# Modulation matmuls four in a row on 1024-column tiles, with loads and stores queued behind chosen weight loads

## The chip, the cores and the metric

The kernel runs on one core of a Trainium2 chip. The metric is the device time of one execution in microseconds. Three runs of the kernel before took 1499.29, 1500.6 and 1502.57 us; the median is 1500.6.

## The reference

One inference step of a two-layer decoder, for a prompt of 512 tokens and 8 sample sequences of 4 tokens. D is 1024. Each of the two layers has a mixer (layer 0: gated convolution and pooling; layer 1: dilated attention and a Conformer convolution) and a ConvFFN. Both are wrapped in RMSNorm and in a shift, scale and gate that come from the conditioning vector c. This modulation is what the change is about:

```python
c_act = jax.nn.silu(c)                       # 9 vectors: 1 prompt, 8 samples
for l in range(DEPTH):
    mod = (c_act @ w["ada_w"][l] + w["ada_b"][l])[:, None, :]   # (9,1024) @ (1024,6144)
    sh1, sc1, g1, sh2, sc2, g2 = jnp.split(mod, 6, axis=-1)
    h = _rmsnorm(x, ng[0]) * (1 + sc1) + sh1
    y, ... = _mixer_ab(h, ...)  or  _mixer_cd(h, ...)
    x = x + g1 * _rmsnorm(y, ng[1])
    h = _rmsnorm(x, ng[2]) * (1 + sc2) + sh2
    y, ... = _conv_ffn(h, ...)
    x = x + g2 * _rmsnorm(y, ng[3])
```

Beside y the outputs hold the convolution and pooling states and the key and value caches; the old cache rows are copied from input to output.

## The kernel before, in words

Activations lie feature by feature: `X`, and the normalized input split in a high and a low part, `Hhi` and `Hlo`, as [128, 8 feature blocks, 2 halves, 272 tokens] (256 prompt tokens and 16 sample tokens per half). A big product (`gemm`, `mm`, lines 527 to 531) is made of blocks of 128 output features. For each of up to 8 input blocks and each half it runs three matmuls of 272 columns: whi by Hhi, whi by Hlo, wlo by Hhi. So one block with 8 input blocks has 48 matmuls. Its weights come in loads of 256 KB into `wraw` (7 buffers, SyncE's DMA queue, line 509); ScalarE makes the high part `whi` (line 510), VectorE or GpSimd the low part `wlo` (line 511), both with 8 buffers, which is 4 blocks of 8. The first and last blocks of some products are run one half at a time.

The modulation is in `ada(l, s)`: for each layer l, a third s of the 6144 columns (2048). It runs over the 8 input blocks k. For each k there are four loads of 128 x 512 (256 KB, line 403) and four matmuls (line 404) with `cact[:, k, :]` (32 columns: 9 vectors and zeros) as the stationary operand, each into its own 32 rows of one PSUM tile. Then the result goes to SBUF (line 407), is turned by four transposes (line 410), and gets its bias and norm weight (line 412 on). 192 loads of 256 KB make up the 50 MB of `ada_w`.

`ada` is a Python generator, and `weave` takes one step of it after each block of a big product. The first third of layer 0 runs at the start, before the input projection; the other two in `mixer0` beside the input and output projections; all of layer 1 in the first ConvFFN, behind `bias_vectors`, which makes the vectors of the attention bias. The tiles of `ada` come from `wraw` at the start, then from six or four buffers of their own. The order of the trace gives priorities, from which a planner with its own costs makes a fixed order for each engine; each engine then works through its queue in that order. Nothing ties a modulation load or a matmul to a place in it.

SyncE issues all DMAs, stores too. `caches` (24 copies, DRAM to DRAM, 27 MB together, line 1207) is traced beside the last ConvFFN; having no inputs to wait for, the copies have their places wherever SyncE is free, in this trace from 103 to 916 us. The key and value stores (line 963) and the bias vectors (line 1200) stand in SyncE's queue and wait there for ScalarE.

At the start `xprep` multiplies X by its norm and `first` applies scale and shift for half 0, then `second` for half 1 after the first three blocks of half 0.

Of the kernel before, what the change touches and what calls it, by code (L numbers as in the profile page):

```python
# [41 lines left out]
XRB = 6  # L42
# [225 lines left out]
def build(nc, tc, ctx, t):  # L268
# [21 lines left out]
    cst = cp.tile([P, NCST], F32, name="cst")  # L290
    cact = cp.tile([P, KB, 32], F32, name="cact")
# [97 lines left out]
    apool = []  # L389

    def ada_tile():
        if apool:
            ap, n = apool[-1]
            return ap.tile([P, CH, HT], F32, name="adaw", bufs=n).rearrange("p a n -> p (a n)")[:, 0:512]
        return wp.tile([P, 512], F32, name="adaw", tag="wraw", bufs=WRAW)

    def ada(l, s):
        ps = psum1("psada")
        for k in range(KB):
            for j in range(4):  # L400
                wt = ada_tile()
# [6 lines left out]
        pt = psum1("psadat")  # L408
# [3 lines left out]
        V.tensor_tensor(  # L412
            mods[l][:, s * 16:s * 16 + 16, :].rearrange("p (j c) n -> p j c n", c=4),
            pt.rearrange("p (c j n) -> p j c n", c=4, j=4)[:, :, :, 0:NMOD],
            par[:, o:o + 16].rearrange("p (j c) -> p j c", c=4).unsqueeze(3).to_broadcast([P, 4, 4, NMOD]),
            op=ADD)

        def ng(i):
            oo = PAR["norm_g"][0] + (l * 4 + i) * KB
            return par[:, oo:oo + KB].unsqueeze(2).to_broadcast([P, KB, NMOD])  # L420

        mb = mods[l]
        if s == 0:
            V.scalar_tensor_tensor(cA[l][0], mb[:, 8:16, :], 1.0, ng(0), op0=ADD, op1=M)
        elif s == 1:
            V.tensor_tensor(cG[l][0], mb[:, 16:24, :], ng(1), op=M)
        else:
            V.scalar_tensor_tensor(cA[l][1], mb[:, 32:40, :], 1.0, ng(2), op0=ADD, op1=M)
            V.tensor_tensor(cG[l][1], mb[:, 40:48, :], ng(3), op=M)
        yield  # L430
# [73 lines left out]
    def load_w(ap, kc, eng):  # L504
# [3 lines left out]
        n = kc * P  # L508
        SY.dma_start(raw[:, :n], ap.rearrange("p k n -> p (k n)"))
# [4 lines left out]
    def load_block(w, n, k0, k1, eng):  # L514
        out = []
        for a in range(k0, k1, 4):
            b = min(a + 4, k1)
            hi, lo = load_w(w[n, :, a:b, :], b - a, eng[a // 4 % 2])
            out += [(hi[:, i * P:(i + 1) * P], lo[:, i * P:(i + 1) * P]) for i in range(b - a)]
        return out  # L520

    def mm(ps, wt, src, h0, h1):
        last = len(wt) - 1
        for i, (whi, wlo) in enumerate(wt):
# [5 lines left out]
            for h in range(h0, h1):  # L530
                PE.matmul(ps[:, h, :HT], wlo, xhi[:, h, :], start=False, stop=(i == last))  # L531
# [86 lines left out]
    def ffn(l, nxt, side, pre):  # L618
# [11 lines left out]
        if l == 0:  # L630
            apool.append((fp, 4))
# [42 lines left out]
        def body():  # L674
# [8 lines left out]
            SY.dma_start(t[f"o_f{l}"], so)  # L683
            yield from down(ng - 1)
            apool.clear()
# [8 lines left out]
    def mixer0(nxt, side, pre, loaded):  # L694
# [5 lines left out]
        apool.append((st0, XRB))  # L700
# [42 lines left out]
        def ev(i, nb, ps, h0, h1):  # L743
            kind, j = divmod(nb, 4)
            if kind == 3:
# [5 lines left out]
                if h1 == 2:  # L751
# [4 lines left out]
                    if j == 3:  # L756
                        SY.dma_start(t["o_b"], ob)
# [6 lines left out]
            elif kind == 2:  # L764
# [5 lines left out]
                z = ap_.tile([P, 562], F32, name="za", bufs=2)  # L770
                conv3(z, ext, pr("a_w")[:, 3 * j:3 * j + 3])
                tmp["z"] = z
            else:
# [7 lines left out]
        weave(gemm(t["w_abi"], order, 0, KB, srcH, ev, lead=LEAD0, mids=(pre, None), loaded=loaded), side, drain=False)  # L781
        SY.dma_start(t["o_a"], oa)
        ea.close()
        er.close()
        apool[-1] = (es.enter_context(pool("mix0w")), 4)
        ey = ExitStack()
        Y = ey.enter_context(pool("mix0y", side="right")).tile([P, KB, 2, HT], F32, name="Y0")
        weave(gemm(t["w_abo"], range(KB), 0, KB, lambda k: (yhi[:, k], ylo[:, k]),
                   out_evac(Y, acc, cG[0][0], True, True), tail=TAIL, mids=(None, lambda: junction(0, Y, acc, nxt))), side)
        es.close()  # L790
        apool.clear()
# [3 lines left out]
    def mixer1(nxt, pre):  # L795
# [41 lines left out]
        def ev_d(i, nb, ps, h0, h1):  # L837
# [12 lines left out]
            if h1 == 2:  # L850
                SY.dma_start(t["o_d"][:, j, 1:9, :], sv[:, :, 4:34])
                SY.dma_start(t["o_d"][:, j, 0, :], ext[:, 512:542])
# [84 lines left out]
        def ev_c(i, nb, ps, h0, h1):  # L937
# [25 lines left out]
            SY.dma_start(t["o_kv"][6 * (kind - 1) + n], kt)  # L963
# [226 lines left out]
    def bias_vectors():  # L1190

        rel = ada_tile()[0:64, 0:12]
        SY.dma_start(rel, t["rel"])
        for c in range(3):
            oh, rv = ada_tile()[0:64, :], ada_tile()[0:12, :]
            SY.dma_start(oh, t["ohp"][:, c * 512:(c + 1) * 512])
            ps = psum1("psrv")
            PE.matmul(ps[0:12, :], rel, oh, start=True, stop=True)
            A.activation(rv, ps[0:12, :], AF.Copy)
            SY.dma_start(rvd[:, c * 512:(c + 1) * 512], rv)  # L1200
            yield

    def caches():
        for g in range(3):
            n = CBATCH[g]
            for b in range(0, DB, n):
                SY.dma_start(t[f"o_c{g}"][b:b + n].rearrange("b w n -> b (w n)").rearrange("b (q n) -> q b n", q=16),
                             t[f"cache{g}"][b:b + n, 4:CW[g]].rearrange("b w n -> b (w n)").rearrange("b (q n) -> q b n", q=16))
# [4 lines left out]
    er = ExitStack()  # L1213
# [74 lines left out]
```

## Time and profile before

| | us |
|---|---|
| median of three runs | 1500.6 |
| profiled execution, device time | 1496.0 |
| its span | 1494.3 |
| TensorE busy | 1417.8 |
| VectorE, ScalarE, GpSimd busy | 882.1, 618.8, 170.6 |
| modulation matmuls (line 404) busy | 102.6 |

The span runs from the first to the last instruction. In the rows below an engine is named PE (TensorE matmul), PEld (its weight loads), DVE (VectorE), ACT (ScalarE), POOL (GpSimd) or SP (SyncE); a "q" behind it is its queue, and L404 is line 404 of the kernel. One fp32 matmul is two instructions. In timelines and in the chain, the first number is the start, the second the time taken, and x is the number of instructions. In rows by stretch, each engine's busy time stands with its count; the last three numbers are the granted TensorE clock as a share of full speed, the share of time for which the 16 DMA engines were busy, and what they moved.

### The profile page before, as it was taken

Reading aid. Unit: us, or ns where it says so; the run is one execution under the profiler, and the core shown is the slowest. Engines: PE = TensorE matmul, PEld = TensorE weight load, DVE = VectorE, ACT = ScalarE, POOL = GpSimd, SP = SyncE. Lnnn points to the kernel's source line nnn. Section 1 sums busy time; section 2 is a strip of 40 time slices with the busy share of each in tenths; the row PEclk is TensorE's granted clock in tenths of the full one; section 3 lists DMA queues with packets and bytes.
Section 4 is the critical chain, followed back from the end, with each engine's and each line's share of the span. In section 5 each row is a group of like instructions: output and inputs, shape, how many; then the busy total and the mean of one; then the engine's idle time right before and its main releaser. Section 6 shows DMA issues by size and latency. Waiting matters only on the chain.

```text
span 1494.3 us, 26853 instructions
## 1 busy us (share of the span) xinstructions
PE 1417.8 (95%) x10354; PEld 1271.0 (85%) x10354; DVE 882.1 (59%) x1788; ACT 618.8 (41%) x1145; POOL 170.6 (11%) x384
## 2 busy tenths in 40 slices
PE   6899997999999999999799999999699999999995
PEld 2578897988798798899699999678599999999995
DVE  1664427753165346446859979652886456456457
ACT  2322235743244234235652442643674444244244
POOL 0210014110011001001500000000521011011011
PEclk9799998999999999999999999999899999999998
DMA  7775633325445546544236245446122332332311
GB/s 264 242 253 187 201 106 100 103 98 180 160 155 194 161 139 212 165 158 186 89 113 197 94 141 178 135 146 239 57 85 69 103 93 71 104 91 65 113 51 61
DMA packets 112633, 207.72 MB, mean 139 GB/s; under 512 B 20884, under 2 KB 33684, under 8 KB 111992
## 3 DMA queue, kind: packets, MB, share of 16 engines
q1 hardware_dynamic: 112504, 206.00, 42.5%
q8 instruction: 81, 1.33, 0.4%
q14 instruction: 48, 0.39, 0.1%
HBM read 198.63 MB, written 34.39 MB: 156 GB/s over the span
## 4 chain that ended last, share of the span: by engine, by line
PE 88%; DVE 6%; DMA 2%; ACT 2%; issue 1%; SPq 0%; POOL 0%; POOLq 0%; DVEq 0%; ACTq 0%
PE psmm L527 23%; PE psmm L531 23%; PE psmm L529 23%; PE psada L404 6%; PE psn L442 2%; PE psmh L529 2%; PE psmh L527 2%; PE psmh L531 2%; PE pso L1013 1%; PE psl L979 1%; PE psl L981 1%; DVE X L492 1%; DVE Yf L491 1%; DVE Y L491 1%; DVE Hlo L481 1%
## 5 line engine op out<-in xcount | busy, mean ns | idle before, releaser
L510 ACT ACTIVATE whi<-wraw 128x512 fp32r<-128x512 f32 (+1 forms) x404 | 239.8, 600 | 511.4 <-PE psmm L529 411.6
L527 PE MATMUL psmm<-Hhi,whi 128*128 128x272 f32 x2028 | 435.9, 291 | 1.0 <-DVE extu L750 1.0
L531 PE MATMUL psmm<-Hhi,wlo 128*128 128x272 f32 x2028 | 431.4, 289 | 0.3 <-POOL wlo L511 0.3
L529 PE MATMUL psmm<-Hlo,whi 128*128 128x272 f32 x2028 | 430.0, 288 | 0.0
L511 DVE TENSOR_TENSOR wlo<-wraw,whi 128x512 fp32r<-128x512 f32 (+1 forms) x374 | 240.8, 649 | 303.4 <-ACT whi L510 288.3
L527 PEld LDWEIGHTS psmm<-Hhi,whi 128*128 128x128 f32 x2028 | 321.4, 189 | 24.3 <-issue 12.6
L529 PEld LDWEIGHTS psmm<-Hlo,whi 128*128 128x128 f32 x2028 | 322.5, 189 | 9.0 <-issue 9.0
L531 PEld LDWEIGHTS psmm<-Hhi,wlo 128*128 128x128 f32 x2028 | 321.5, 189 | 9.9 <-issue 9.2
L527 PE MATMUL psmm<-act_hi,whi 128*128 128x272 f32 x624 | 135.5, 290 | 0.0
L531 PE MATMUL psmm<-act_hi,wlo 128*128 128x272 f32 x624 | 135.3, 289 | 0.0
L529 PE MATMUL psmm<-act_lo,whi 128*128 128x272 f32 x624 | 132.7, 288 | 0.0
L578 DVE SCALAR_TENSOR_TENSOR fz<-fext,par,fz 128x560 f32<-128x560 f32 x88 | 70.5, 801 | 74.3 <-ACT fz L577 74.2
L404 PE MATMUL psada<-adaw,cact 128*32 128x512 f32 x384 | 102.6, 628 | 8.3 <-DMA adaw<-ada_w 8.3
L527 PEld LDWEIGHTS psmm<-act_hi,whi 128*128 128x128 f32 x624 | 99.6, 188 | 11.8 <-issue 8.4
L531 PEld LDWEIGHTS psmm<-act_hi,wlo 128*128 128x128 f32 x624 | 99.6, 188 | 7.6 <-issue 7.5
L529 PEld LDWEIGHTS psmm<-act_lo,whi 128*128 128x128 f32 x624 | 99.1, 188 | 0.8 <-issue 0.8
L577 ACT ACTIVATE fz<-fext,par 128x560 f32<-128x560 f32 x88 | 75.2, 855 | 34.5 <-DVE fext L647 34.5
L874 DVE SCALAR_TENSOR_TENSOR zd<-extd,par,zd 128x512 f32<-128x512 f32 x120 | 87.0, 746 | 0.7
L569 POOL COPY fso<-fext 128x2 f32<-128x2 f32 x88 | 23.1, 263 | 530.6 <-ACT fext L646 530.6
L579 DVE SCALAR_TENSOR_TENSOR fz<-fext,par,fz 128x560 f32<-128x560 f32 x88 | 70.5, 801 | 2.7
L646 ACT ACTIVATE fext<-psmm 128x512 f32<-128x512 f32 (+1 forms) x88 | 49.7, 564 | 51.1 <-PE psmm L531 51.1
L527 PE MATMUL psmh<-Hhi,whi 128*128 128x272 f32 x148 | 48.2, 326 | 16.1 <-ACT Hhi L479 14.5
(260 smaller groups left out, 1692.9 us busy)
## 6 DMA issues: line engine op xcount, KB each, us to landing
adaw<-ada_w SPq DMA_DIRECT2D x192, 256.0 KB, 3.6
wraw<-w_up SPq DMA_DIRECT2D x176, 256.0 KB, 3.0
wraw<-w_dn SPq DMA_DIRECT2D x64, 256.0 KB, 2.8
o_c<-cache SPq DMA_DIRECT2D x8, 2040.0 KB, 10.0
wraw<-w_cdi SPq DMA_DIRECT2D x52, 256.0 KB, 4.6
wraw<-w_abi SPq DMA_DIRECT2D x32, 256.0 KB, 4.5
o_c<-cache SPq DMA_DIRECT2D x8, 1016.0 KB, 7.1
kc<-kc SPq DMA_DIRECT2D x28, 256.0 KB, 3.7
```

Of the source, the lines that this page charges most:

```text
L404: PE.matmul(ps[32 * j:32 * j + 32, :], cact[:, k, :], wt, start=(k == 0), stop=(k == KB - 1))
L442: PE.matmul(ps, ones, a, start=(i == 0), stop=(i == n - 1))
L510: A.activation(hi[:, :n], raw[:, :n], AF.Copy)
L511: eng.tensor_tensor(lo[:, :n], raw[:, :n], hi[:, :n], op=SUB)
L527: PE.matmul(ps[:, h, :HT], whi, xhi[:, h, :], start=(i == 0), stop=False)
L529: PE.matmul(ps[:, h, :HT], whi, xlo[:, h, :], start=False, stop=False)
L531: PE.matmul(ps[:, h, :HT], wlo, xhi[:, h, :], start=False, stop=(i == last))
L577: A.activation(z[:, :n], ext[:, 2:2 + n], AF.Identity, bias=b, scale=w[:, 2:3])
L578: V.scalar_tensor_tensor(z[:, :n], ext[:, 1:1 + n], w[:, 1:2], z[:, :n], op0=M, op1=ADD)
L579: V.scalar_tensor_tensor(z[:, :n], ext[:, 0:n], w[:, 0:1], z[:, :n], op0=M, op1=ADD)
L646: A.activation(fpr(ext, 2, h0, h1), cpr(ps, h0, h1), AF.Copy)
L874: V.scalar_tensor_tensor(cpr(z), ip, dw[:, i:i + 1], cpr(z), op0=M, op1=ADD)
```

## The change

The parts of the diff, in order. `ada` works on halves (l, s, q) of 256 columns per matmul. One load of 512 KB brings four operands, [128, 2, 512]; there are 96 such loads in place of 192. The four matmuls are traced together, and `issue_after(newest[0])` puts them behind the last matmul of the newest block. The tiles have four buffers (start and mixer 0) or three (first ConvFFN). Evacuation and bias go by halves, and the four transposes become two matmuls with a selection of 36 columns, `ssel`. `queued()` puts a DMA behind the newest weight load: modulation loads, bias inputs, cache copies and state stores. The projections' weaving is new: in mixer 0 two tiles per step, all beside the input projection; in the ConvFFN one tile, with 4 steps for 3 tiles; cache copies every third step. The key and value stores and the bias vectors are issued by ScalarE. At the start the normalized X lies in the norm's four buffers, for half 1 made in `second`'s place.

```diff
-XRB = 6
+ADB = (4, 3)
...
+    ssel = cp.tile([P, 4, NMOD], F32, name="ssel")
+    apool = [st0]
+    newest, loaded_w = [], []
+    def queued():
+        return tc.issue_after(loaded_w[0]) if loaded_w else nullcontext()
     def ada_tile():
-        if apool:
-            ap, n = apool[-1]
-            return ap.tile([P, CH, HT], F32, name="adaw", bufs=n).rearrange("p a n -> p (a n)")[:, 0:512]
-        return wp.tile([P, 512], F32, name="adaw", tag="wraw", bufs=WRAW)
-    def ada(l, s):
-        ps = psum1("psada")
-        for k in range(KB):
-            for j in range(4):
-                wt = ada_tile()
-                o = s * 2048 + j * 512
-                SY.dma_start(wt, t["ada_w"][l, k, :, o:o + 512])
-                PE.matmul(ps[32 * j:32 * j + 32, :], cact[:, k, :], wt, start=(k == 0), stop=(k == KB - 1))
-            yield
-        ev = np_.tile([P, 512], F32, name="adaev", tag="nsq", bufs=NSQ)
+        return apool[-1].tile([P, 2, 512], F32, name="adaw", bufs=ADB[len(apool) - 1])
+    def ada(halves, per, ahead):
+        todo = [(l, s, q, k) for l, s, q in halves for k in range(KB)]
+        tiles = []
+        def load():
+            if todo[len(tiles):]:
+                l, s, q, k = todo[len(tiles)]
+                tiles.append(ada_tile())
+                with queued():
+                    SY.dma_start(tiles[-1], t["ada_w"][l].rearrange("k p (s a q n) -> s q k p a n", s=3, a=2, q=2)[s, q, k])
+        for _ in range(ahead):
+            load()
+        for i, (l, s, q, k) in enumerate(todo):
+            load()
+            if k == 0:
+                ps = psum1("psada")[:, 0:256]
+            wt = tiles[i]
+            with tc.issue_after(newest[0]) if newest else nullcontext():
+                for j in range(4):
+                    PE.matmul(ps[32 * j:32 * j + 32, :], cact[:, k, :], wt[:, j // 2, 256 * (j % 2):256 * (j % 2) + 256],
+                              start=(k == 0), stop=(k == KB - 1))
+            if k == KB - 1:
+                ada_out(l, s, q, ps)
+            if i % per == per - 1:
+                yield
+    def ada_out(l, s, q, ps):
+        if q == 0 and l == 0 and s == 0:
+            V.tensor_copy(ssel, ident.rearrange("p (j n) -> p j n", j=4)[:, :, 0:NMOD])
+        ev = wp.tile([P, 256], F32, name="adaev", tag="wraw", bufs=WRAW)
         A.activation(ev, ps, AF.Copy)
-        for c in range(4):
-            PE.transpose(pt[:, c * P:(c + 1) * P], ev[:, c * P:(c + 1) * P], ident)
+        for c in range(2):
+            PE.matmul(pt[:, :, c, :], ev[:, c * P:c * P + P], ssel, start=True, stop=True)
...
-        SY.dma_start(raw[:, :n], ap.rearrange("p k n -> p (k n)"))
+        loaded_w[:] = [SY.dma_start(raw[:, :n], ap).ins]
...
-                PE.matmul(ps[:, h, :HT], wlo, xhi[:, h, :], start=False, stop=(i == last))
+                x = PE.matmul(ps[:, h, :HT], wlo, xhi[:, h, :], start=False, stop=(i == last))
+        newest[:] = [x.ins]
...
-            SY.dma_start(t["o_kv"][6 * (kind - 1) + n], kt)
+            A.dma_start(t["o_kv"][6 * (kind - 1) + n], kt)
...
+            A.dma_start(rvd[:, c * 512:(c + 1) * 512], rv[c])
...
+                with queued():
+                    SY.dma_start(t[f"o_c{g}"][b:b + n]...
...
+            XR[h, c] = np_.tile([P, CH, HT], F32, name="xr", tag="nsq", bufs=NSQ)
...
-    a = ada(0, 0)
+    a = ada([(0, 0, 0), (0, 0, 1)], 2, 2)
...
-    pre = mixer0((0, 1), chain(delay(1), pace(chain(ada(0, 1), ada(0, 2)), 7, 8)),
-                 second, loaded)
-    pre = ffn(0, (1, 0), chain(delay(8), bias_vectors(), slow(chain(ada(1, 0), ada(1, 1), ada(1, 2)), 2)), pre)
+    pre = mixer0((0, 1), chain(delay(1), ada([(0, i, q) for i in (1, 2) for q in range(2)], 2, 0)),
+                 lambda: (xprep(1), first(1, 0, KB)), loaded)
+    pre = ffn(0, (1, 0), chain(delay(8), bias_vectors(), pace(ada([(1, i, q) for i in range(3) for q in range(2)], 1, 0), 3, 4)), pre)
     pre = mixer1((1, 1), pre)
-    ffn(1, None, caches(), pre)()
+    ffn(1, None, slow(caches(), 3), pre)()
```

## Rows read from the trace of the kernel before

**Rows 1.** The page, parts 1 and 4: span, TensorE's busy time, chain by line.
```profile
span 1494.3 us, 26853 instructions
PE 1417.8 (95%) x10354; PEld 1271.0 (85%) x10354; DVE 882.1 (59%) x1788; ACT 618.8 (41%) x1145; POOL 170.6 (11%) x384
PE psmm L527 23%; PE psmm L531 23%; PE psmm L529 23%; PE psada L404 6%; PE psn L442 2%; PE psmh L529 2%; PE psmh L527 2%; PE psmh L531 2%; PE pso L1013 1%; PE psl L979 1%; PE psl L981 1%; DVE X L492 1%; DVE Yf L491 1%; DVE Y L491 1%; DVE Hlo L481 1%
```

**Rows 2.** TensorE's waits: line <- releaser: us in total, times, longest.
```profile
PE psada L404 <- DMA adaw<-ada_w: 8.3, 3, 4.1
...
PE psmm L531 <- POOL wlo L511: 0.3, 1, 0.3
```

**Rows 3.** Line 404 by stretch: length, PE, PEld busy (count), clock, DMA share, GB/s.
```profile
61.30:195.00 133.70, 27.49 (x128) 3.89 (x128) 1.00 0.65 212
325.00:640.00 315.00, 51.84 (x192) 7.17 (x192) 1.00 0.53 175
```

**Rows 4.** TensorE's timeline from 61 us, line 404: first and last of 75.
```profile
61.35 1.06 PE L404 MATMUL psada<-adaw,cact 128*32 128x512 f32 x6
...
637.13 1.07 PE L404 MATMUL psada<-adaw,cact 128*32 128x512 f32 x8
```

**Rows 5.** Chain of waits from 110 us: start, us, work, instructions in it.
```profile
117.47 0.99 PE psada L404 x8
118.46 0.45 PE psmm L527 x2
118.91 0.25 PE psmm L529 x2
...
124.64 0.44 PE psadat L410 x4
```

**Rows 6.** The same chain from 334 us: one modulation matmul alone.
```profile
334.68 0.97 PE psada L404 x2
335.66 0.32 PE psmm L529
```

**Rows 7.** The same chain from 1026 us: 256-column matmuls of the sample attention.
```profile
1026.44 0.57 PE psr L1157 x8
1027.01 0.45 PE psmm L527 x2
...
1033.78 1.00 PE psr L1157 x16
...
1035.98 0.80 PE psys L1168 x8
```

**Rows 8.** Stretches: length, PE, PEld, DVE, ACT, POOL, clock, DMA share, GB/s.
```profile
2.00:22.00 20.00, 15.05 (x40) 4.37 (x40) 0.00 (x0) 4.44 (x9) 0.00 (x0) 1.00 1.03 351
22.00:34.00 12.00, 9.28 (x38) 3.55 (x38) 6.43 (x12) 3.01 (x6) 0.00 (x0) 1.00 0.45 145
34.00:47.50 13.50, 8.25 (x22) 1.97 (x22) 1.69 (x11) 2.79 (x5) 3.60 (x7) 0.75 0.94 325
47.50:61.30 13.80, 10.94 (x48) 9.54 (x48) 13.24 (x39) 8.63 (x18) 5.53 (x4) 0.63 0.54 174
1100.00:1456.00 356.00, 356.00 (x2858) 356.00 (x2857) 206.26 (x385) 155.26 (x250) 42.77 (x127) 1.00 0.30 88
```

**Rows 9.** SyncE's timeline: modulation loads issued around 18 us.
```profile
17.93 14.28 SPq L403 DMA_DIRECT2D adaw<-ada_w  x8
```

**Rows 10.** VectorE's timeline: two products of X and its norm for half 1.
```profile
64.25 1.36 DVE L1224 TENSOR_TENSOR xr<-X,nr 128x544 f32<-128x544 f32 x2 [1.06 <-PE psada L404]
```

**Rows 11.** Waits of SyncE's queue: line <- releaser: us, times, longest.
```profile
SPq L403 <- PE psada L404: 243.7, 80, 22.4
...
SPq L963 <- ACT kt L960: 75.0, 12, 17.5
```

**Rows 12.** DMA issues by line: count, KB each, median us to landing.
```profile
vc<-vc SPq DMA_DIRECT2D x14, 512.0 KB, 6.9
```

**Rows 13.** Line 963, issue of the key and value stores: ns min/median/max, first and last start.
```profile
L963 SPq DMA_DIRECT2D o_kv<-kt x12: 332/338/352, 760.8 to 921.1; - x12
```

More of the change, by code (lines that the diff above doesn't have):

```diff
@@ L682, in body @@
                 yield from up(e + 1, FGROUPS[gi + 1][1])
-            SY.dma_start(t[f"o_f{l}"], so)
-            yield from down(ng - 1)
-            apool.clear()
+            for i, _ in enumerate(down(ng - 1)):
+                if i == 3:
+                    with queued():
+                        SY.dma_start(t[f"o_f{l}"], so)
+                yield
+            del apool[1:]
         weave(body(), side)
@@ L780, in mixer0 @@
         order = ABI
-        weave(gemm(t["w_abi"], order, 0, KB, srcH, ev, lead=LEAD0, mids=(pre, None), loaded=loaded), side, drain=False)
-        SY.dma_start(t["o_a"], oa)
+        weave(gemm(t["w_abi"], order, 0, KB, srcH, ev, lead=LEAD0, mids=(pre, None), loaded=loaded), side)
+        with queued():
+            SY.dma_start(t["o_b"], ob)
+            SY.dma_start(t["o_a"], oa)
         ea.close()
         er.close()
-        apool[-1] = (es.enter_context(pool("mix0w")), 4)
         ey = ExitStack()
         Y = ey.enter_context(pool("mix0y", side="right")).tile([P, KB, 2, HT], F32, name="Y0")
-        weave(gemm(t["w_abo"], range(KB), 0, KB, lambda k: (yhi[:, k], ylo[:, k]),
-                   out_evac(Y, acc, cG[0][0], True, True), tail=TAIL, mids=(None, lambda: junction(0, Y, acc, nxt))), side)
+        for _ in (gemm(t["w_abo"], range(KB), 0, KB, lambda k: (yhi[:, k], ylo[:, k]),
+                   out_evac(Y, acc, cG[0][0], True, True), tail=TAIL, mids=(None, lambda: junction(0, Y, acc, nxt)))):
+            pass
         es.close()
-        apool.clear()
         return lambda: (junction(1, Y, acc, nxt), ey.close())
@@ L1190, in bias_vectors @@
     def bias_vectors():
-        rel = ada_tile()[0:64, 0:12]
-        SY.dma_start(rel, t["rel"])
+        bt = [ada_tile() for _ in range(3)]
+        rel, rv = bt[1][0:64, 1, 0:12], [bt[2][0:12, 0, :], bt[2][0:12, 1, :]]
+        with queued():
+            SY.dma_start(bt[0][0:64], t["ohp"][:, 0:1024].rearrange("p (a n) -> p a n", a=2))
+            SY.dma_start(bt[1][0:64, 0, :], t["ohp"][:, 1024:1536])
+            SY.dma_start(rel, t["rel"])
+        yield
+        yield
+        rv.append(ada_tile()[0:12, 0, :])
         for c in range(3):
-            oh, rv = ada_tile()[0:64, :], ada_tile()[0:12, :]
-            SY.dma_start(oh, t["ohp"][:, c * 512:(c + 1) * 512])
             ps = psum1("psrv")
-            PE.matmul(ps[0:12, :], rel, oh, start=True, stop=True)
-            A.activation(rv, ps[0:12, :], AF.Copy)
-            SY.dma_start(rvd[:, c * 512:(c + 1) * 512], rv)
+            with tc.issue_after(newest[0]):
+                PE.matmul(ps[0:12, :], rel, bt[c // 2][0:64, c % 2, :], start=True, stop=True)
+            A.activation(rv[c], ps[0:12, :], AF.Copy)
+            A.dma_start(rvd[:, c * 512:(c + 1) * 512], rv[c])
             yield
@@ L1212, in build, with xstat, xprep @@
     warm(cact[:, 0, 0:1])
-    er = ExitStack()
-    st0 = er.enter_context(pool("mix0r", side="right"))
     XR = {}
-    def xprep(h, c0, c1):
-        if c0 == 0:
-            XR[h] = rstd(squares(h), onesD)
-        r = XR[h].unsqueeze(1).to_broadcast([P, CH, HT])
-        for c in range(c0, c1, CH):
-            XR[h, c] = st0.tile([P, CH, HT], F32, name="xr", tag="adaw", bufs=XRB)
+    def xstat(h):
+        XR[h] = rstd(squares(h), onesD)
+    def xprep(h):
+        r = XR.pop(h).unsqueeze(1).to_broadcast([P, CH, HT])
+        for c in range(0, KB, CH):
+            XR[h, c] = np_.tile([P, CH, HT], F32, name="xr", tag="nsq", bufs=NSQ)
             V.tensor_tensor(XR[h, c], X[:, c:c + CH, h, :], r, op=M)
```

66 lines of the change are left out of this document (29 added, 37 removed).

## The prediction

> **What bounds the kernel now.** I read the page's parts 1 and 4 first: TensorE is busy 1417.8 us of a 1494.3 us span, and the chain that ended last lies on it for 88%, of which 6% is line 404, the modulation matmuls [rows 1]. So what a matmul takes is paid almost in full, and a faster DMA or vector step pays only where TensorE idles. TensorE's own waits come second. Modulation matmuls wait 8.3 us in 3 places for their weights, and the big products wait 0.3 us for a split weight [rows 2]: behind the start nothing that SyncE loads is late. Third, line 404 by stretch: 128 of its 384 instructions lie in layer 0's input projection and 192 in layer 0's ConvFFN, in both of which the granted clock is 1.00 [rows 3]; the other 64 belong to the start. Last, the start: the DMA engines move 351 GB/s up to 22 us, only 145 GB/s from there to 34, and 325 up to 47.5; then, up to 61.3 us, TensorE runs 48 matmul records where a full stream at 0.125 us each (two take 0.25 [rows 5]) would need 6.0 of 13.8 us [rows 8].
>
> **What one modulation batch costs.** Four matmuls of 32 output columns each use separate column groups and run side by side. Eight instructions (four matmuls in a row) take 0.99 us on the chain, and the pair of big matmuls behind them takes 0.45 instead of 0.25 [rows 5]: 1.19 us. A single one takes 0.97, and the matmul behind it 0.32 instead of 0.125 [rows 6]: 1.17 us. One alone costs what four cost. After the start the timeline has 75 such batches, from 61.35 to 637.13 us [rows 4], for 160 matmuls: 20 are whole fours, 5 are threes, 15 pairs and 35 single ones. 26 lie in the input projection, 49 in the ConvFFN. At 1.18 us that is 88.5 us.
>
> **The change, part by part.**
> *Four in a row, 256 columns each.* One 512 KB tile now holds the four operands, so all four become ready together, and the order to stand behind a block's last matmul keeps them from cutting into it. After the 16 batches of the start there are 80. The nearest rows are the sample attention's, with the same 32-column groups and the same 256 moving columns: a four takes 0.57 and the pair behind it 0.45, so 0.77 us; two fours in a row take 1.00, so 1.20 with the pair behind [rows 7]. In the ConvFFN one batch goes at a time: 48 x 0.77 = 37.0 us. In the input projection two go per step: 16 x 1.20 = 19.2. Together 56.2 us, a gain of 32.3. Were no two adjacent, 80 x 0.77 = 61.6, gain 26.9. Were a 256-column four as dear as today's 1.17, 93.6, a loss of 5.1; I take the rows with the same shape.
> *The fold.* Four transposes (0.44 us [rows 5]) become two matmuls of 36 columns per half, 10 pairs behind the start where 5 fours stood. Four matmuls of 16 columns take 0.80 [rows 7], so a pair about 0.40, plus 0.1 for the change of shape: 10 x 0.50 - 5 x 0.44 = +2.8 us. Ends: 0, and +10 if a pair costs as much as 1.2 us. The halved evacuations (12 on ScalarE, more small adds on VectorE) lie beside matmuls; those engines are busy 41% and 59% [rows 1].
> *The start.* The hole from 22 to 34 us is TensorE's doing: eight loads take 14.28 us to issue [rows 9], as each waits for a buffer that a lone matmul (1 us) must free, with the norm's matmuls in between. Now a batch frees 512 KB in well under the 1.5 us that 512 KB takes at 351 GB/s, so the loads set the pace. The 13.1 MB moved up to 47.5 us (20 x 351 + 12 x 145 + 13.5 x 325, in GB/s times us [rows 8]) would take 37.5 us at 351, 8 us less. The first half's modulation is done eight tiles earlier, so half of the first pre-norm work can come before the end of the loads: I take 2 of the 7.8 us lost after 47.5. Against it, half 1's normalized X loses two of its early buffers: two more products, 1.36 us [rows 10], and some reshuffling, -2. Sum -8 us. Ends: 0 (the hole stays, filled by other waits) and -16 (all 8 and all 7.8).
> *Loads pinned behind weight loads.* In SyncE's queue, in order, whatever stands behind a load that waits for its buffer waits too. Today such waits come to 243.7 us [rows 11] and TensorE feels none of it. With four buffers and two tiles per step, a modulation load can go two blocks ahead: 2 x (48 x 0.125 + 1.2) = 14.4 us, of which the next block's weights, queued behind it, need 6.9 us to land, as a 512 KB load does [rows 12], and some 3 us to be split: some 5 us spare. The traffic is 1.57 MB per 7.2 us, 218 GB/s, against 212 now [rows 3] and 351 shown [rows 8]. In the ConvFFN three tiles at 4/3 blocks each give four blocks, over 20 us. I charge 2 us for hiccups; ends 0, and 35 if each of the 64 steps is late by 0.55.
> *Cache copies into the last ConvFFN, state stores later.* 27 MB move into a stretch in which TensorE is busy 356.0 of 356 us and DMA stands at 0.30 [rows 8]: some 90 GB/s more over 72 of its 88 steps, on top of 88. Taking them away elsewhere frees nothing TensorE waits for. 0 us; if their cover fails, weight loads there come late.
> *ScalarE's own stores.* SyncE's queue stood 75.0 us for 12 of them [rows 11]; nobody on TensorE waited. 15 issues of about 0.34 us [rows 13] go to ScalarE, with evacuations queued behind them; exposed in full that is 5 us, beside matmuls 0.
> Sum: -32.3 + 2.8 - 8 + 2 = -35.5 us. The profiled execution took 1496.0 us (span 1494.3 and 1.7 around it), so 1460.5 for its like; the median of the runs shown is 1500.6, so the forecast is 1465.
>
> **A rule weighed.** The granted clock was 0.75 from 34 to 47.5 us and 0.63 behind it, a mix of 2.4 and 1.2 GHz; in the first of these stretches TensorE was busy 8.25 of 13.5 us [rows 8]. The Trainium skill, "TensorE: Matmul & The Clock Gate", section "HAM oscillation", says that short bursts between DMA waits bring the slow clock back each time, and it speaks against this change: a TensorE that is faster in the start idles more there. In direction this trace agrees, by the two clocks just named. By my sum the start gives 8 us; by the rule it gives about 4 (rival 2).
>
> **Rivals.**
> 1. *Pinned loads become the bound.* Place: SyncE's queue in the input projection, where the spare is 5 us and VectorE splits weights between other work. A weight late by x costs x in each step; from 0.55 us per step over 64 steps the gain is gone. At 1 us a step: 1465 + 64 - 2 = 1527, slower. Against: 0.3 us of weight waits today [rows 2], traffic hardly above today's. 7%.
> 2. *The start gives little.* Either TensorE goes through the start at 1.2 GHz: the first three blocks' 72 matmuls would cost 9 us more at half clock, of which the 13.8 us at a mean of 0.63 already hold some 5, so 4 lost, 1469; or the norm's matmuls still block the batches, 1473. For it: the norm's squares wait for X as before. 20%.
> 3. *The start gives all.* -16 instead of -8: 1457. For it: VectorE works 13.24 of the 13.8 us behind the loads [rows 8], and half of that could move ahead. 10%.
> 4. *The change doesn't do what it says:* something readier is put between the four. Split in two, 160 x 0.77 = 123 us instead of 56: 1532. Against: one load wakes all four. 3%.
>
> **How the numbers follow.** The forecast (gains of line 404 and the start near the sum) has 60%: 1465, its own range 1458 to 1473. Rivals 2 and 3 lie beside it, rivals 1 and 4 are slower (10%, of which 2% may be no change at a mild lateness). The range takes the lower end from rival 3 and the unpaired batches with little from the start (1465 + 5.4 + 8) plus some lateness as the upper: 1452 to 1483. Faster than 0.2% (3 us, about what a measurement can tell from no change) 0.90, within it 0.02, slower 0.08.
>
> **What would show it.** Line 404 after the start: 48 lone groups of eight instructions near 0.57 us and 16 pairs near 1.00, none of two instructions. The last modulation load landing near 37 to 40 us, with no hole in GB/s. TensorE's waits still without DMA or weight rows beyond a few us. The last ConvFFN still at full business. Wrong would be: rows of line 404 waiting for DMA behind the start, matmuls waiting for wlo or whi, batches near 1 us each, or an input projection that is not some 10 us and a ConvFFN that is not some 20 us shorter.

## The result and the profile after

The changed kernel takes 1577.7 us (median of 4 runs, 1576.4 to 1578.9) against 1499.9 for the kernel before: ratio 1.0519, 95% interval 1.0497 to 1.0541. It is 78 us slower; 1465 was forecast, 35 us faster.

The page's span and busy times of the changed kernel:

```profile
span 1575.8 us, 27444 instructions
PE 1432.6 (91%) x10762; PEld 1319.8 (84%) x10762; DVE 885.2 (56%) x1803; ACT 612.1 (39%) x1151; POOL 159.2 (10%) x384
```

TensorE is busy 15 us more than before [rows 1], but 143 us of the span are idle, where it was 76. Its own waits, the first by total and the modulation's:

```profile
PE psmm L554 <- ACT whi L537: 38.6, 12, 4.9
PE psmm L558 <- DVE wlo L538: 19.3, 23, 1.2
...
PE psada L426 <- DMA adaw<-ada_w: 11.4, 10, 5.4
PE psadat L440 <- ACT adaev L437: 11.3, 11, 3.5
```

The split weights, for which TensorE waited 0.3 us before [rows 2], now cost 58 us. No load stands beside them: all of line 426's waits for loads lie before 38 us.

For the stages I cut each kernel at five marks: the first pooling matmul of the input projection, and the first normalized product of each junction (VectorE's Y from Y and nr). Lengths in us:

| | start | first mixer | first ConvFFN | second mixer | last ConvFFN | median |
|---|---|---|---|---|---|---|
| before | 82.3 | 146.0 | 487.0 | 338.3 | 417.7 | 1499.9 |
| changed | 66.5 | 150.8 | 484.3 | 349.6 | 501.8 | 1577.7 |

Behind the last mark some 23 us follow in both. The marks do not cut the work alike: in the changed kernel 40 records of big matmuls fewer lie in the first ConvFFN (3172, before 3212) and 40 more in the second mixer. At 0.125 us each that is 5 us. At equal work the first ConvFFN is 2.3 us longer than before, not 2.7 shorter, and the second mixer 6.3 us longer, not 11.3. Stage lengths below are by the marks; "at equal work" says that they were set right in this way.

The loss lies in the last ConvFFN, +84.1 us: the stage in which the forecast put nothing but the cache copies, at 0 us. The stretches of the changed kernel (columns as in [rows 8]) are the start, most of the first mixer and of the first ConvFFN, and of the last:

```profile
0.00:22.00 22.00, 10.88 (x69) 3.39 (x70) 0.31 (x3) 5.96 (x9) 0.46 (x9) 1.00 0.94 319
22.00:34.00 12.00, 11.38 (x80) 6.70 (x79) 6.88 (x19) 5.68 (x10) 0.00 (x0) 1.00 0.85 288
34.00:47.50 13.50, 6.52 (x38) 4.64 (x35) 12.80 (x40) 6.89 (x14) 5.06 (x8) 0.62 1.03 381
...
66.50:217.20 150.70, 145.58 (x1211) 133.71 (x1211) 65.30 (x131) 43.95 (x81) 11.19 (x21) 0.99 0.50 168
...
290.00:701.50 411.50, 399.59 (x3187) 367.45 (x3186) 199.14 (x393) 148.61 (x258) 26.78 (x112) 0.98 0.42 135
...
1100.00:1553.00 453.00, 402.58 (x2961) 395.80 (x2960) 215.56 (x421) 159.66 (x272) 34.19 (x127) 0.92 0.37 126
```

In the last row TensorE is idle for 50.4 us, and its granted clock is 0.92. Before, the same work (1100 to 1471 us) was 370.9 busy of 371.2 at 1.00. So of the 84 us 50 are idle and 32 are slower matmuls.

How one stop comes about shows in ScalarE's timeline of the changed kernel (start, duration, instruction, in brackets the idle time before it and who ended it):

```profile
1212.42 0.60 ACT L674 ACTIVATE fext<-psmm 128x512 f32<-128x512 f32 x1 [4.13 <-PE psmm L558]
1213.41 0.85 ACT L605 ACTIVATE fz<-fext,par 128x560 f32<-128x560 f32 x1 [0.39 <-DVE fext L675]
1215.97 0.67 ACT L686 ACTIVATE fz<-fz 128x560 f32<-128x560 f32 x1 [1.71 <-DVE fz L607]
1216.55 3.21 ACT L537 ACTIVATE whi<-wraw 128x512 fp32r<-128x512 f32 x6
```

and in TensorE's beside it:

```profile
1211.92 0.40 PE L558 MATMUL psmm<-Hhi,wlo 128*128 128x272 f32 x2
1217.21 0.82 PE L554 MATMUL psmm<-Hhi,whi 128*128 128x272 f32 x2 [4.89 <-ACT whi L537]
...
1219.36 0.82 PE L558 MATMUL psmm<-Hhi,wlo 128*128 128x272 f32 x2 [0.87 <-DVE wlo L538]
```

Six splits of weights (3.21 us) stand in ScalarE's queue behind the evacuation, convolution and gate of the block that TensorE has just finished. Their data is there: nothing stands in brackets. TensorE can't start the next block until that whole evacuation is through. ScalarE meanwhile waits 4.13 us for TensorE, with the six splits behind the waiting instruction. It happens ten times (37.0 of the 38.6 us), five times for 4.9 us and five times for 2.5, mostly some 25 us apart. VectorE's low parts stand in sixes too, and TensorE waits 13.1 us in 15 places of that stage for them. Loads do come late to ScalarE there, which they did not in the kernel before (its waits from 1051.2 to 1553 us):

```profile
ACT whi L537 <- DMA wraw<-w_dn: 16.2, 6, 4.6
ACT whi L537 <- DMA wraw<-w_up: 6.8, 3, 5.2
```

But all nine of these waits lie between the stops, while TensorE works; none of the ten stops has one in it. In the kernel before the same engine takes its splits singly, between the evacuations:

```profile
1136.71 0.85 ACT L577 ACTIVATE fz<-fext,par 128x560 f32<-128x560 f32 x1 [0.56 <-DVE fext L647]
1138.01 0.63 ACT L510 ACTIVATE whi<-wraw 128x512 fp32r<-128x512 f32 x1 [0.45 <-PE psmm L529]
1141.00 0.63 ACT L510 ACTIVATE whi<-wraw 128x512 fp32r<-128x512 f32 x1 [2.35 <-PE psmm L529]
1141.54 0.58 ACT L646 ACTIVATE fext<-psmm 128x512 f32<-128x512 f32 x1
```

After each of the ten stops the clock is at 0.50, the lower of its two levels (1.2 and 2.4 GHz). Stretches of the changed kernel around the first:

```profile
1213.00:1217.00 4.00, 0.00 (x0) 0.00 (x0) 2.12 (x4) 1.90 (x4) 0.58 (x3) 0.72 0.00 2
1217.00:1219.00 2.00, 1.28 (x4) 0.95 (x4) 1.97 (x6) 2.00 (x5) 0.00 (x0) 0.50 0.00 0
...
1221.00:1223.00 2.00, 2.00 (x11) 2.00 (x10) 1.32 (x3) 0.00 (x0) 0.00 (x0) 0.50 0.90 259
1223.00:1225.00 2.00, 2.00 (x11) 2.00 (x11) 0.00 (x0) 0.00 (x0) 0.00 (x0) 0.50 0.99 264
1225.00:1227.00 2.00, 2.00 (x18) 2.00 (x18) 0.00 (x0) 0.00 (x0) 0.00 (x0) 1.00 1.47 580
```

From 1221 to 1225 us a 2 us stretch holds 11 matmuls instead of 18. Behind the ten stops TensorE works for 3 to 8 us at 0.50; the 32 us are some 3 us for each stop. The Trainium skill, "TensorE: Matmul & The Clock Gate", section "HAM oscillation", says of a kernel whose matmuls wait for DMAs that after each such wait they start at the slow clock again. Here the waits are for ScalarE's splits; this trace agrees, at 0.50.

### The profile page after: what moved, and what is told of

Read it like the earlier page. It is cut to its first block, busy times and chain, and to the rows that moved or that the text cites. A ratio compares the mean times of both kernels' runs of the same rounds, so it can differ in the third digit from the quotient of the medians.

```text
span 1575.8 us, 27444 instructions
## 1 busy us (share of the span) xinstructions
PE 1432.6 (91%) x10762; PEld 1319.8 (84%) x10762; DVE 885.2 (56%) x1803; ACT 612.1 (39%) x1151; POOL 159.2 (10%) x384
## 4 chain that ended last, share of the span: by engine, by line
PE 82%; DVE 10%; ACT 4%; DMA 2%; issue 1%; POOL 0%; SPq 0%; DVEq 0%; POOLq 0%; ACTq 0%
PE psmm L558 22%; PE psmm L554 22%; PE psmm L556 21%; PE psada L426 3%; PE psn L469 3%; PE psmh L554 2%; PE psmh L556 1%; PE psmh L558 1%; PE pso L1043 1%; DVE wlo L538 1%; DMA kc<-kc 1%; PE psl L1009 1%; PE psl L1011 1%; DVE X L519 1%; ACT fz L605 1%
## 5 line engine op out<-in xcount | busy, mean ns | idle before, releaser
L554 PE MATMUL psmm<-Hhi,whi 128*128 128x272 f32 x2028 | 450.3, 299 | 33.7 <-ACT whi L537 33.7
L558 PE MATMUL psmm<-Hhi,wlo 128*128 128x272 f32 x2028 | 444.0, 296 | 13.5 <-DVE wlo L538 13.5
L556 PE MATMUL psmm<-Hlo,whi 128*128 128x272 f32 x2028 | 442.3, 295 | 0.0
L554 PEld LDWEIGHTS psmm<-Hhi,whi 128*128 128x128 f32 x2028 | 334.3, 196 | 55.2 <-ACT whi L537 37.1
L558 PEld LDWEIGHTS psmm<-Hhi,wlo 128*128 128x128 f32 x2028 | 333.9, 195 | 19.1 <-DVE wlo L538 17.6
L556 PEld LDWEIGHTS psmm<-Hlo,whi 128*128 128x128 f32 x2028 | 334.5, 195 | 1.6 <-issue 1.4
L606 DVE SCALAR_TENSOR_TENSOR fz<-fext,par,fz 128x560 f32<-128x560 f32 x88 | 70.5, 801 | 70.8 <-ACT fz L605 70.5
L675 DVE COPY fext<-psmm 128x32 f32<-128x32 f32 (+1 forms) x88 | 16.5, 188 | 142.2 <-ACT fext L674 140.9
L605 ACT ACTIVATE fz<-fext,par 128x560 f32<-128x560 f32 x88 | 75.2, 854 | 28.6 <-DVE fext L675 27.8
L621 DVE TENSOR_TENSOR Yf<-psmm,Yf 128x544 f32<-128x544 f32 x32 | 23.2, 724 | 89.1 <-PE psmm L558 89.1
L426 PE MATMUL psada<-adaw,cact 128*32 128x256 f32 x768 | 61.7, 412 | 11.4 <-DMA adaw<-ada_w 11.4
```

What stands on the lines that cost most here:

```text
L426: PE.matmul(ps[32 * j:32 * j + 32, :], cact[:, k, :], wt[:, j // 2, 256 * (j % 2):256 * (j % 2) + 256], start=(k == 0), stop=(k == KB - 1))
L554: PE.matmul(ps[:, h, :HT], whi, xhi[:, h, :], start=(i == 0), stop=False)
L556: PE.matmul(ps[:, h, :HT], whi, xlo[:, h, :], start=False, stop=False)
L558: x = PE.matmul(ps[:, h, :HT], wlo, xhi[:, h, :], start=False, stop=(i == last))
L605: A.activation(z[:, :n], ext[:, 2:2 + n], AF.Identity, bias=b, scale=w[:, 2:3])
L606: V.scalar_tensor_tensor(z[:, :n], ext[:, 1:1 + n], w[:, 1:2], z[:, :n], op0=M, op1=ADD)
```

## The experiments

Theory A: the cache copies, queued behind chosen weight loads, change the order of ScalarE's instructions in the last ConvFFN, which is fixed before the run, and this order alone is the loss. Rival B: the copies' bytes make the weight loads there late. Rival C: another part of the change does it.

**1. The pinned copies alone.**

```diff
 before.py
+    with queued():                     # behind the newest weight load
         SY.dma_start(t[f"o_c{g}"]..., t[f"cache{g}"]...)
-    ffn(1, None, caches(), pre)()
+    ffn(1, None, slow(caches(), 3), pre)()
```

> The kernel before with one part of the change: the 24 cache copies go behind weight loads in SyncE's queue, one in three steps of the last ConvFFN. Theory A (order: the planner prices a 2 MB copy as a long stop of SyncE's queue, takes the six weight loads behind it for late, and fixes ScalarE's order with their splits behind the next blocks' evacuations; TensorE then waits for that order): the last ConvFFN takes 453 us instead of 371, total 1500 + 82 = 1582. Theory B (traffic: the copies' bytes hold up the weight loads on the chip): the same 1582. Theory C (the loss comes from another part, such as the modulation edits or ScalarE's own stores): 1500.

Measured: 1550.3 us, ratio 1.0335 (1.0313 to 1.0356). The last ConvFFN takes 503.4 us (+85.7) and shows the same ten stops, so C is out for that stage. TensorE's waits for whi there:

```profile
PE psmm L531 <- ACT whi L514: 37.0, 10, 4.9
```

The total is 32 us under the 1582 expected, for the first ConvFFN takes 454.0, 33 less than before (30 at equal work), with the modulation code untouched. Its line 408 in the stretch of the second row of [rows 3]:

```profile
325.00:640.00 315.00, 23.44 (x176) 3.46 (x176) 1.00 0.49 154
```

23.4 us where there were 51.8 (the other 16 instructions lie before 325 us). In the order of TensorE's instructions all 24 groups of four matmuls in that stage are now whole; before, 49 batches did the same work. So it was the copies, spread over that stage in the kernel before, that had taken the fours apart. 25 batches less, at the forecast's 1.18 us, are 29.5 us, which is the 30 at equal work.

**2. The change with its copies as before.**

```diff
 after.py
-    with queued():
-        SY.dma_start(t[f"o_c{g}"]..., t[f"cache{g}"]...)
+    SY.dma_start(t[f"o_c{g}"]..., t[f"cache{g}"]...)
-    ffn(1, None, slow(caches(), 3), pre)()
+    ffn(1, None, caches(), pre)()
```

> The changed kernel with the copies traced as in the kernel before: not pinned, one per step. A and B: the last ConvFFN is back at 371 us, total 1577.7 - 82 = 1496. C: 1577. If the copies, now placed by the planner into the first ConvFFN, put splits late there too (four bunches of seven in ScalarE's order), up to 15 us of that are lost again: 1496 to 1511.

Measured: 1499.8 us, ratio 0.9998 (0.9983 to 1.0013); last ConvFFN 418.7. The pinned copies are the whole 78 us, and with the copies where they were the rest of the change is worth nothing.

**3. The copies in the same stretch from GpSimd's queue.**

```diff
 after.py
-    with queued():
-        SY.dma_start(t[f"o_c{g}"]...
+    with tc.issue_after(newest_g[0]):  # GpSimd's newest state store
+        G.dma_start(t[f"o_c{g}"]...
```

> The changed kernel with the same copies in the same stretch, but issued by GpSimd, each behind its latest state store; ScalarE's order then has the splits in ones and twos again. This tells A from B: the bytes stay in the last ConvFFN, the order doesn't. A: the last ConvFFN at 371 to 380 us, total 1496 to 1505. B: still near 453 us, total 1570 to 1580.

Measured: 1536.8 us, ratio 1.0245 (1.0224 to 1.0267); last ConvFFN 464.4: between what was expected of A and of B. With the same bytes there TensorE waits for no weight any more, which speaks against B. Half of the loss stays, under other names (waits of TensorE in that stage):

```profile
PE psmm L554 <- DVE fext L675: 12.8, 5, 7.2
PE psmm L554 <- DVE act_hi L610: 11.6, 2, 5.8
PE psmh L554 <- DVE act_hi L610: 6.1, 2, 5.2
```

They wait for evacuations now. GpSimd fills the state rows that these need, and its queue holds the copies' issues too. That this is the link I infer; no run parts it.

**4. The splits ahead of the evacuations, copies as in the change.**

```diff
 after.py, gemm(), in the last ConvFFN only
+    for n in range(i, i + 4): wts[n] = load_block(...)   # three blocks ahead
     mm(ps, wts.pop(i), src, 0, 2)
+    with tc.issue_after(loaded_a[0]), tc.issue_after(loaded_v[0]):
         evac(i, blocks[i], ps, 0, 2)   # behind the newest split
```

> The changed kernel with the copies where they are, in SyncE's queue, but in the last ConvFFN the weights of three blocks ahead are traced first, and a block's evacuation is tied behind the newest split on ScalarE and VectorE. Only the order is changed; queue and bytes stay. A: most of the waits go, the ConvFFN at 375 to 400 us, total 1498 to 1523 (bunches stay where a product begins). B: weights still land late and TensorE waits for them with a DMA row behind it, total 1560 or more.

Measured: 1540.1 us, ratio 1.0267 (1.0243 to 1.0291); last ConvFFN 463.2: again between A and B. The waits for whi fall to 24.3 us in five places from 37.0 in ten, and the stage loses 45.5 us instead of 84.1. Five stops in place of ten leave about half the loss.

**5 and 6. The copies in the second mixer**, issued by GpSimd, in the changed kernel and in the kernel before.

```diff
-    SY.dma_start(t[f"o_c{g}"]...
+    with tc.issue_after(G.tensor_copy(cpin, newhi[0][:, 0:1]).ins):
+        G.dma_start(t[f"o_c{g}"]...
-    pre = mixer1((1, 1), pre)
+    pre = mixer1((1, 1), pre, pace(caches(), 5, 4))
     ...
+    ffn(1, None, iter(()), pre)()
```

> The changed kernel, but its cache copies are issued by GpSimd, each behind the newest weight load, in the second mixer and no longer in the last ConvFFN, whose weight splits then stand in the order of the kernel before. If the order of the splits is the whole loss of the last ConvFFN, that stage takes 418 us (before 417.7, changed kernel 501.8) and the kernel 66.6 + 151 + 484 + 348 + 418 + 23 = 1490 us. If another part of the change costs in that stage too, it stays at 430 us or more and the time at 1505 or more. If the copies' 16.8 MB themselves cost where they run, the second mixer is longer than 360 us.

> The kernel before, with the cache copies alone moved: issued by GpSimd in the second mixer, so that they break neither the fours of the ada batches in the first ConvFFN nor the order of the splits in the last. If whole fours are worth what the pinned copies alone showed there (first ConvFFN 487 to 454 us), the kernel takes 1499 - 33 = 1466 us, with the last ConvFFN at 418. If that gain came from somewhere else than the copies' leaving the first ConvFFN, it stays at 1499.

(The copies are 27 MB, eight each of 2040, 1016 and 248 KB, not the 16.8 given there.) Measured: 1558.1 us, ratio 1.0383 (1.0363 to 1.0403), and 1529.9, ratio 1.0208 (1.0185 to 1.0232): both misses in the total. The last ConvFFN is right (419.9 and 418.9), the first too (483.9 and 456.9), but the second mixer takes 410.1 and 403.0, which is 60.5 and 64.7 us more than in the two kernels without the move; a cost of the copies where they run was the third case of 5. In experiment 6:

```profile
PE pssl L1071 <- DMA kc<-kc: 21.5, 9, 5.4
PE psvt L934 <- ACT kt L961: 19.3, 1, 19.3
```

Here transfers do come late: TensorE waits for the key caches themselves, which it waited 1.7 us for before. So the copies have a price in this stage, where a product reads its loads directly. Why kt comes late in the second row no run parts.

**7. As 5, with the fold one step later.**

```diff
+    if late and k == late[1]:
+        ada_out(*late[0]); late = None
     if k == KB - 1:
-        ada_out(l, s, q, ps)
+        late = ((l, s, q, ps), per - 1)   # the start's two halves stay as they were
```

> As the changed kernel with its copies in the second mixer, and each fold of an ada half (ScalarE's copy, the four small matmuls, VectorE's additions) comes one step later than its last matmul. If TensorE's waits for ScalarE's copy (11.3 us in all, 11 waits) are what the change's ada loses in the mixer and the first ConvFFN, this is 8 to 11 us under the same kernel with the fold at once. If the late splits in the same stretch (VectorE and ScalarE, 12 us) come of the order and not of the fold, the gain is under 4 us.

Measured: 1533.6 us, 24.5 less than 5, over twice what was expected. First mixer 143.3 (151.0), first ConvFFN 467.6 (483.9; at equal work 14.9 less). Stretch 290 to 678.7 us, TensorE's busy time and clock:

```profile
290.00:678.70 388.70, 386.62 (x3154) 356.86 (x3153) 196.44 (x386) 147.05 (x254) 30.34 (x110) 1.00 0.44 142
```

2.1 us idle at clock 1.00, where the changed kernel has 11.9 at 0.98. The late splits of that stage go with the fold's wait.

**8. As 5, with the modulation loads not queued behind chosen loads.**

> As the changed kernel with its copies in the second mixer, and its ada loads not queued behind chosen weight loads (issued when a buffer is free). If the order after a chosen load costs the first ConvFFN its late splits, that stage falls from 484 to about 470 us and the total by 10 to 15. If not, the total is the same within 3 us; if the order is what keeps the batches apart, it is slower, as the batches crowd.

Its diff takes away `with queued():` in the modulation's load(). Measured: 1588.0 us, 30 slower than 5; first mixer 159.0, first ConvFFN 503.9. From 225.6 to 729.5 us TensorE waits for whi five times:

```profile
PE psmm L556 <- ACT whi L538: 22.4, 5, 5.4
```

The same stop again, in another stage. With the copies in the second mixer, queueing those loads behind weight loads was right.

**9. The change with copies of 16 rows**, queued as they were.

```diff
-    SY.dma_start(t[f"o_c{g}"][b:b + n]..., t[f"cache{g}"][b:b + n, 4:CW[g]]...)
+    SY.dma_start(t[f"o_c{g}"][b:b + n, 0:16]..., t[f"cache{g}"][b:b + n, 4:20]...)
```

> The changed kernel with its 24 cache copies queued behind the same chosen weight loads, but of 16 rows each (32 KB); the other rows are left out. The splits of the last ConvFFN then stand in the order of the kernel before (ones and twos). If the order is the loss, that stage takes 418 us and the kernel 1494. If being queued behind a chosen load is itself the loss, the stage stays near 500 and the kernel near 1577. (A gain here can't part the order from the bytes; the copies on GpSimd's queue, which had all bytes and no wait for a weight, part these.)

Measured: 1492.6 us, ratio 0.9952 (0.9933 to 0.9971); last ConvFFN 421.0, splits in ones and twos again. Being queued behind a chosen load is not the loss. With the same code, the copy's size alone changes the order that is written out for ScalarE before the run. That the planner reckons with it as a transfer's time is the likely reason; no run shows it.

**10. The kernel before, copies from ScalarE in the last ConvFFN.**

```diff
 before.py
+    with tc.issue_after(loaded_a[0]):  # behind the newest split
+        A.dma_start(t[f"o_c{g}"]...
```

> The kernel before with the copies alone moved: in the last ConvFFN, issued by ScalarE, each behind the newest weight split there, with all their bytes. ScalarE's order there has five runs of six splits, where the copies pinned on SyncE's queue gave eight of six and one of ten, and the kernel before none over two. If the long runs of splits are what stops TensorE, the last ConvFFN loses 5/9 of 85 us, about 47, and the kernel takes 1499 - 33 + 47 = 1513 us. If it is the copies' presence in that stage, it takes 1550 as with the copies pinned on SyncE's queue; if only the load queue's own order counts, 1466.

Measured: 1487.2 us, ratio 0.9913 (0.9886 to 0.9939). Last ConvFFN 440.6, a loss of 23 where 47 was expected: between the cases named, and the length of the runs is a poor measure: five runs of six splits stand there, and TensorE waits for whi once, for 1.2 us. What counts, it seems, is whether the splits that TensorE needs next stand behind an evacuation; no run parts that. What the run does show: all 27 MB in that stage, on a queue whose order stays near the old one, cost at most 23 us, and the first ConvFFN is again 454.5.

**11 and 12. Copies as in experiment 2, the fold late; then also two batches at a time in the first ConvFFN.**

```diff
-    pace(ada([(1, i, q) for i in range(3) for q in range(2)], 1, 0), 3, 4)
+    pace(ada([(1, i, q) for i in range(3) for q in range(2)], 2, 0), 3, 8)   # 12 alone
```

> The changed kernel with the copies issued as in the kernel before and each fold one step later than its last matmul. From 1499.8 us (copies as before) the late fold takes 8 us in the first mixer and 16 in the first ConvFFN, as in the second mixer's run: 1476 us, under both kernels. If the late fold's gain there hung on the copies' being out of the first ConvFFN, 1495 or more.

> As the run with the copies as before and the late fold, and in the first ConvFFN the ada batches come two at a time at half the rate (about half of them stay whole as 16 matmuls in a row). If the switch between the modulation matmuls and the main ones costs what the batches' rows say (two batches of eight 2 x 0.77 us, one of sixteen 1.2 us), 12 whole pairs save about 4 us: 1472. If a late fold or a late load behind the pair takes it back, the same or slower.

Measured: 1493.1 us, ratio 0.9951 (0.9934 to 0.9969), and 1473.5, ratio 0.9823 (0.9802 to 0.9844). Number 12 is faster than both kernels, 1.8% below the one before. Number 11 misses: the late fold gives 7 us in the first mixer and nothing in the first ConvFFN (486.5), where TensorE still waits 11.0 us for splits. With the copies going through that stage, splits are late whether the fold is late or not. In number 12 the stage takes 469.8:

```profile
290.00:684.70 394.70, 388.14 (x3179) 363.02 (x3179) 200.32 (x393) 151.17 (x259) 30.68 (x111) 0.99 0.54 188
```

Idle 6.6 us against 13.3 in number 11; 14 whole pairs at 2 x 0.77 - 1.20 give 4.8 us; the clock, 0.99 for 0.98, is some 4 of 400 us by my estimate. With the idle time that is 15 of the 16.7 us that the stage gains on number 11, four times what was expected of the pairs. So the total of 1472 was met by luck: number 11 stayed 17 us above its forecast, and the pairs gave as much more.

**13. The order alone**, with the copies of experiment 9.

```diff
 as 9, in the last ConvFFN
+    silu[:] = [A.activation(zg..., AF.Silu).ins]; held[0] = 6 if every second gate
+    with tc.issue_after(silu[0]) if held[0] else nullcontext():
         A.activation(hi[:, :n], raw[:, :n], AF.Copy)
```

> As the changed kernel with copies of 16 rows each (the other rows are left out), which left the last ConvFFN at 421 us. Now ScalarE's order alone is made bad there: after every second gate the next six splits are queued behind that gate's own ScalarE work, which puts eleven runs of 8 to 11 splits into its order (the changed kernel had eight of 6 and one of 10). No bytes are added. If the order is the cause, TensorE stops once in each of the eleven places for about 5 us (as in the changed kernel, 50 us of idle in 10 places) and its clock falls again, so the stage takes 475 to 510 us and the kernel 1545 to 1580. If the copies' bytes are needed for the loss, the stage stays under 435 and the kernel under 1508.

Measured: 1573.8 us, ratio 1.0469 (1.0443 to 1.0496); last ConvFFN 500.5. The stretch of that stage, and one of the stops:

```profile
1096.00:1550.00 454.00, 398.13 (x2972) 395.41 (x2971) 219.26 (x424) 164.84 (x278) 27.57 (x128) 0.91 0.23 71
...
1239.87 0.82 PE L557 MATMUL psmm<-Hhi,whi 128*128 128x272 f32 x2 [5.16 <-ACT whi L539]
```

71 GB/s instead of 126, and yet the same kind of idle (55.9 us), nearly the same clock and 80 us lost against experiment 9. The idle time is that of eleven stops, as expected. So an order of this kind makes a loss of this size without the bytes, which is what A claims. It is not the changed kernel's own order; there the waits themselves (37.0 + 13.1 of 50.4 us of idle are for splits, none of the stops for a load) say the same.

**14. The copies in the first ConvFFN from ScalarE, fold late, batches in pairs.**

```diff
 as 12
+    with tc.issue_after(loaded_a[0]):
+        A.dma_start(t[f"o_c{g}"]...
+    pre = ffn(0, (1, 0), both(chain(delay(4), slow(caches(), 3)), chain(delay(8), ...)), pre)
```

> As the run with the late fold and the ada batches in pairs, but with the copies issued by ScalarE behind the newest weight split, one per three steps of the first ConvFFN, where the splits' order then has no run over six and the pairs stay whole (20 of 24, before 11). If whole pairs and few late splits are what is left to gain in that stage, it goes from 470 to 459 us and the kernel from 1473.5 to 1461. If the copies' bytes beside the ada's cost there, or their issues on ScalarE stop it as they did in the last ConvFFN (440.6 for 417.7), 1480 or more.

Measured: 1486.3 us, ratio 0.9900 (0.9881 to 0.9918): the second case, not the gain hoped for. 23 pairs stay whole, and still the first ConvFFN takes 486.8: it is idle for 14.2 of the 400 us from 290 to 690, at a clock of 0.98. Late splits and, for the first time there, other small waits are among its rows. Why, this run does not say.

## Why the prediction was wrong

**Cache copies into the last ConvFFN: the step that failed.** The forecast put 0 us, with "if their cover fails, weight loads there come late". The loss is 84 us, and TensorE waited there for no load. I costed the copies as traffic beside a TensorE that is never idle [rows 8]; what they changed was the order in which ScalarE takes its work. TensorE's 356.0 of 356 us [rows 8] hung on splits standing singly between evacuations, and I had not looked at ScalarE's order, only at its busy share of 41%. Experiments 1 and 2 place the loss, 3 and 9 part bytes from order, 13 makes one of its size by the order alone. "Taking them away elsewhere frees nothing TensorE waits for" was wrong too: their place in the first ConvFFN had broken its fours, 27 to 30 us at equal work (experiments 1, 6 and 10).

**The rivals.** Two signs named for a wrong forecast came: matmuls waiting for whi and wlo, and a first ConvFFN that is not some 20 us shorter. Rival 1 had the mark to look for, matmuls waiting for whi or wlo, but another place (input projection) and another cause (a late load); no DMA wait of line 426 stands behind the start. Rival 4 did not happen: all batches are whole.

**Batch prices: right, what they are set against: not.** The chain of the changed kernel in the input projection and in the first ConvFFN:

```profile
108.87 1.00 PE psada L426 x16
109.87 0.45 PE psmm L554 x2
...
406.58 0.57 PE psada L426 x8
407.15 0.46 PE psmm L554 x2
```

These are the 1.20 and 0.77 us of the forecast, in 48 lone groups, as forecast. In the first ConvFFN line 426 and the fold are busy 30.7 + 3.8 us where the old lines had 51.8 [rows 3] and, for the fold, 1.8: 19 less, as summed. But the 49 batches that the gain was counted from hung on the copies, which the change moves as well. With the copies gone the old tiles give 24 whole fours (experiment 1), at 1.19 us 28.6 us, where 48 of the new at 0.77 take 37.0. In this stage the new tiles are then a loss: with the fold late it takes 471 us at equal work (experiment 7), with the old tiles 457 (experiment 1).

**The fold: sized at 2.8, measured at some 22 more.** I priced its small matmuls (3.8 us busy for 1.8 in the first ConvFFN, near enough) and put ScalarE's copy beside them. TensorE waits for that copy, 7.8 us in 10 places behind the start, and splits behind it come late. Between experiments 5 and 7, which differ by the fold alone, lie 7.7 us in the first mixer and, at equal work, 14.9 in the first ConvFFN. With the late fold and the copies in the second mixer, the first ConvFFN is 15.8 us shorter than before at equal work, against 19 by the forecast's sum; with the fold's first form it was 2.3 longer.

**Start and first mixer: 18 forecast, 11.0 measured.** The mark between them lies differently in the two kernels (131 big matmul records before it in the one, 120 in the other), so they are read together: 228.2 us to the first junction before, 217.2 after, 211.1 with the late fold. -8 for the start, -11.5 for 26 batches made into 16 pairs and +1 for the fold come to -18.4; -17.1 is measured once the fold is late. Of that 1 to 4 us may be the copies': in experiments 1, 6 and 10, with the old modulation, the first junction comes at 224.4 to 227.3 us. The hole in the loads is gone (288 GB/s from 22 to 34 us, 145 before [rows 8]). The clock is 0.62 from 34 to 47.5 us, lower than before, in the direction of rival 2; that rival's 4 us less is not seen in the total with the late fold.

**Loads behind weight loads: +2, neither shown nor refuted.** Without it the same kernel is 30 us slower (experiment 8).

**ScalarE's stores: 0.** The second mixer is 6.3 us longer than before at equal work in the changed kernel, 0.7 in experiment 12 with the same stores, and 1.4 in experiment 1 with the old ones. No wait for a key or value store stands among TensorE's rows; I did not isolate this, and it stays open.

Sum: the two profiled executions lie 81.5 us apart (the medians 78), 117 more than the -35.5 forecast. The last ConvFFN has 84.1 of that, the fold 22.6, the second mixer 6.3; 4 us stay open.

## What to carry to other kernels

Before moving work off a bottleneck engine's queue, read the order in which the engines that feed it take their instructions: an engine that is 41% busy stops TensorE when the split that TensorE needs next stands behind one evacuation too many, though the data to be split was there long before. A transfer that no one waits for is not free where its size changes the planned order; a change to it is to be costed by comparing orders, not bytes. And when matmul batches cost the same alone as in fours, find what takes the fours apart before building new tiles: here moving the copies alone gave 30 us in the stage that the whole change, copies moved too, left 2 us longer.

## What the runs showed of the hardware

A stop of TensorE costs more here than its own length. In the changed kernel's last ConvFFN ten stops of 2.5 or 4.9 us, with 13 us of waits for low parts beside them, make 50 us of idle; behind each stop the granted clock is 0.50 for 3 to 8 us of work, in which 11 matmuls go in 2 us where 18 do at full clock, and that makes 32 us more. 27 MB of DRAM-to-DRAM copies cost the changed kernel about 7 us where SyncE's queue spreads them over the stages before the second mixer (experiment 2 against 9, all bytes against nearly none). In the second mixer they cost 60.5 and 64.7 us (experiments 5 and 6), with 21.5 us of waits in experiment 6 for the key caches that TensorE reads directly.
